# A two-layer hybrid trunk on one core: copying all of c out of its bank at once, and the row of rstd as two float32r products

## The chip, the cores and the metric

One Trainium2 chip, one core of it. The time is the device time of one launch in microseconds (us), the median of several runs. Beside it stands one profiled execution, from which every row of a trace in this document comes unless another kernel is named. The engines are called PE (TensorE, matrix products), DVE (VectorE), ACT (ScalarE), POOL (GpSimd) and SP (SyncE, which issues most transfers).

## What is computed

A trunk of two layers over 512 tokens of width 1024, all in float32. Each layer normalises its input, makes one combined projection of 3488 columns, feeds four groups of heads with it, multiplies each group's output by a SiLU gate, and projects back. Shortened from the reference:

```python
def hybrid_layer(x, ...):
    h = rmsnorm(x, norm_g)
    p = h @ w_in                                    # 512 x 3488
    (cq, ckv, kr, g_a, c_h, c_b, c_c, g_b, sg_u, sg_v, g_c, mq, mk, mv, g_d) = split(p)
    # A: latent attention, 4 heads; widths of cq, ckv, kr: 256, 128, 32
    q  = (rmsnorm(cq, mla_q_norm_g) @ mla_w_uq)     # 4 x 96
    kv = (rmsnorm(ckv, mla_kv_norm_g) @ mla_w_ukv)  # 4 x (64 + 64)
    k_rope = rope(rmsnorm(kr, mla_k_rope_g))
    ...
    o_a = causal_attention(q, k, v_a)
    o_b = c_b * short_conv(c_c * c_h, conv_w)       # B: width 3
    o_c = spatial_gate(sg_u, sg_v, ...)             # C: causal mixing in chunks of 128
    o_d = moba_attention(qd, kd, vd)                # D: blocks of 256, 4 heads
    y = concat([o_a*silu(g_a), o_b*silu(g_b), o_c*silu(g_c), o_d*silu(g_d)])
    return y @ w_out

def reference(x, ...):
    for l in range(2):
        x = x + hybrid_layer(x, ...)
    return x
```

## The kernel before

**Products.** A float32 operand is split into a high part in float32r and a low part, the rest, also float32r. A product of two such operands is three float32r products: high·high, low·high, high·low (names in the trace: `whi_`/`wlo_` for weights, `hTh`/`hTl` for the transposed input, `cTh`/`cTl` for transposed c). The high part is usually a copy on ACT, the low part a subtraction on DVE. A weight of 512 KB goes through the pool of `raw_` tiles, is split by halves, and waits there for its product. A few products are made in plain float32.

**The order of the work.** Nothing is left to an automatic scheduler. The program has a planner of its own, class `Order`: each piece of work is a generator (`Chain`) that yields due times, a heap picks the earliest, and the instruction is emitted when the planner's clock for its engine gets there. The clocks run on costs written in the program; there is one for each of ACT, DVE, POOL and the transfers, and `o.now` is the time of PE. So the order in which instructions stand on every engine is fixed when the program is built, and it changes as a whole if an operation is added, removed or made longer. All operations of ACT, DVE and POOL are emitted at one line, 178, and all products at line 208; the trace tells them apart by the names of their tiles. Buffers are handed out by `Slots` with `get` and `put`; `shared(slots, n)` is a `put` that acts at its n-th call. There are three accumulator banks of PSUM (`accS`), two for transposes and small things (`trS`), three for scores and other outputs (`sS`), and eleven SBUF tiles of 128x512 (`t2S`).

**Layer 0's beginning.** x is transposed in eight pieces on PE and split. Its norm is applied late: the projections are made of the unnormalised x (times the norm's gain), and the reciprocal root rstd, one number for each token, is multiplied onto what comes out. `x_stats` (line 765) sums the squares on ACT and makes rstd on POOL as a 128x4 array, token within a block by block. `x_row` (line 785) needs it along the free axis and on all partitions: POOL multiplies four identity blocks by the four columns of rstd (tile `rd`, 128x512), PE multiplies a block of ones with it (`rrow`, one float32 product of 512 columns), and ACT copies the bank, halved, to `rh` and its square behind it. `rh` is read by the gates and other outputs of layer 0. `ROWT`, 36,000 ns on the planner's clock, is when this is due.

**The low-rank part, c.** In layer 0 `c_first` (line 1704) makes the 416 columns of cq, ckv and kr for all four blocks of 128 tokens in four banks, three of `accS` and one of `sS`:

```python
home = [accS, accS, accS, sS]
...
if k == KT - 1:
    o.spawn(low_chain(L, t, a[t], o.now + PELAT, home[t]))
```

The banks fill in the order of the blocks, 0 and 1 together, then 2, then 3. For each of them `low_chain` (line 983) copies 384 columns to an SBUF tile `ct`, transposes them in three blocks (`cT`), splits the result (`cTh` on ACT, `cTl` on DVE) and makes q (six products of 384 columns) and kv (three of 512). Beside it `low_stats` (line 953) reads the same bank: three squares on ACT with their sums (32, 128 and 256 columns) and a copy of the last 32 columns to `krt`, on ACT too. The bank goes back when both are through with it. After that come small operations, a reciprocal root on POOL, and `krt`, scaled on DVE; when the last block is there, it is rotated and copied into K. The first product that asks for the first free bank of `accS` is `sq`, the projection of 512 columns to sg_v and mq, whose first split weights lie in the buffer `yTh`, `yTl`.
In layer 1 the same two functions run with one block at a time in `accS`.

**Behind that**, layer 0 runs the gates and projections of all groups between the attention heads: for each head of A scores (`sa`), a scaled and masked exponential (`pa`), transposes (`pTa`), a split (`pha`, `pla`) and the product with v (`oa`); for D the same with `sd`, `pd`, `pTd`, `phd`, `pld`, `od`. `gd` is D's gate, `zz` the product of c_c and c_h for the short convolution, and `oz`, `ox`, `oy` are the output projections, made as products of sums of blocks (as are layer 1's projections to sg_v, mq, mk and mv), with weights such as `whi_b`, `wlo_b`.

The functions that the change touches, with the line numbers of the profile:

Of the kernel before, what the change touches and what calls it, by code (L numbers as in the profile page):

```python
# [11 lines left out]
F32 = mybir.dt.float32  # L12
# [6 lines left out]
P = 128  # L19
S = 512  # L20
# [200 lines left out]
def hybrid_trunk(ctx: ExitStack, tc: tile.TileContext, x, positions, norm_g, w_c, w_f, w_t, w_o, mla_q_norm_g,  # L221
# [501 lines left out]
    xhi, xlo = ([Event() for _ in range(KT)] for _ in range(2))  # L723
    xsum = cst.tile([P, NT, KT // 2], F32, name="xsum")
    xv = cst.tile([P, 4, NT], F32, name="xv")
    v_ev, r_ev, rh_ev = Event(), Event(), Event()
    rh_box, rh_put = [], shared(hS, 14)
    RV, RR, RE, REE = range(4)
# [36 lines left out]
    def x_stats():  # L765
        ch = Chain(o)
        for kp in range(KT // 2):
            yield from ch.wait(xk_ev[2 * kp + 1])
            for t in range(NT):
                yield from ch.act(A.activation, junk[:, 0:2 * P], xk[kp][:, t, :], AF.Square, scale=D ** -0.5,  # L770
                                  accum_out=xsum[:, t, kp:kp + 1])
            c2 = Chain(o, ch.t)
            yield from c2.wait(xk_tr[2 * kp + 1])
            v4S.put(c2)
        yield from ch.dve(V.tensor_reduce, xv[:, RV, :], xsum, axis=AX.X, op=ALU.add)
        yield from ch.dve(V.tensor_scalar, xv[:, RV, :], xv[:, RV, :], 1.0, EPS, op0=ALU.mult, op1=ALU.add)
        t0 = ch.t
        for i, f in ((RE, EPS), (REE, EPS * EPS)):
            yield from ch.dve(V.tensor_scalar, xv[:, i, :], xv[:, RV, :], f, None, op0=ALU.mult)
        o.set(v_ev, ch.t)  # L780
        c2 = Chain(o, max(t0, ROWT))
        yield from pow_rstd(c2, xv[:, RR, :], xv[:, RV, :], NT)
        o.set(r_ev, c2.t)

    def x_row():

        ch = Chain(o)
        yield from ch.wait(r_ev)
        d = yield from t2S.get(ch, "rd")
        yield from ch.pool(G.tensor_tensor, d.rearrange("p (t c) -> p t c", t=NT),  # L790
                           ident.unsqueeze(1).to_broadcast([P, NT, P]),
                           xv[:, RR, :].unsqueeze(2).to_broadcast([P, NT, P]), op=ALU.mult)
        tp = yield from trS.get(ch, "rrow")
        yield from ch.pe(4 * cost(S), PE.matmul, tp, one_box[0][:, 0:P].bitcast(F32), d, start=True, stop=True)
        zz_put(ch)
        t2S.put(ch)
        rh_box.append((yield from hS.get(ch, "rh")))
        yield from ch.act(A.activation, rh_box[0][:, 0:S], tp, AF.Copy, scale=0.5)
        yield from ch.act(A.activation, rh_box[0][:, S:2 * S], tp, AF.Square, scale=0.5)
        trS.put(ch)  # L800
        o.set(rh_ev, ch.t)
# [149 lines left out]


    def low_stats(L, t, a, t0, done):
        ch = Chain(o, t0)
        ssq, krt = L.ssq, L.krt
        ct = L.ct[t]
        for i, (c0, c1) in enumerate(((384, 416), (256, 384), (0, 256))):
            yield from ch.act(A.activation, junk[:, :c1 - c0], a[:, c0:c1], AF.Square, scale=(c1 - c0) ** -0.5,
                              accum_out=ssq[:, t, 2 - i:3 - i])
        yield from ch.act(A.activation, krt[:, t, :], a[:, 384:416], AF.Copy)  # L960
        done(ch)
        m = sm.tile([P, 8], F32, tag="ms", name=f"ms{t}_{L.l}")
        e1, e2 = EPS, EPS * EPS
        if L.l == 0:
            yield from ch.wait(v_ev)
            e1, e2 = rv(RE, t), rv(REE, t)
        yield from ch.dve(V.tensor_scalar, m[:, 0:2], ssq[:, t, 1:3], 1.0, e1, op0=ALU.mult, op1=ALU.add)
        yield from ch.dve(V.tensor_scalar, L.e2[:, t, :], ssq[:, t, 0:2], EPS, e2, op0=ALU.mult, op1=ALU.add)
        yield from pow_rstd(ch, m[:, 4:6], m[:, 0:2], 2)
        L.ms[t] = m  # L970
        o.set(L.stat[t], ch.t)
        yield from ch.dve(V.scalar_tensor_tensor, krt[:, t, :], in0=krt[:, t, :], scalar=m[:, 5:6], in1=L.gr,
                          op0=ALU.mult, op1=ALU.mult)
        L.kr_left -= 1
        if L.kr_left:
            return
        yield from ch.wait(rope_ev)
        yield from rope(ch, krt, 16, cosT, sinT, f"k{L.l}")
        yield from ch.wait(L.QK_ev)
        yield from ch.pool(G.tensor_copy, L.K[:, :, :, 64:96], krt.unsqueeze(2).to_broadcast([P, NT, 4, 32]))  # L980
        o.set(L.kr_ev, ch.t)

    def low_chain(L, t, a, t0, slots):
        ch = Chain(o, t0)
        l = L.l
        done = shared(slots, 2)
        ct = yield from t2S.get(ch, f"ct{t}_{l}")
        L.ct[t] = ct
        o.spawn(low_stats(L, t, a, t0, done))
        if o.clk["A"] < o.clk["V"]:  # L990
            yield from ch.act(A.activation, ct[:, :384], a[:, :384], AF.Copy)
        else:
            yield from ch.dve(V.tensor_copy, ct[:, :384], a[:, :384])
        done(ch)
        tp = yield from trS.get(ch, f"cT{t}_{l}")
        for k in range(3):
            yield from ch.pe(109.0, PE.transpose, tp[:, k * P:(k + 1) * P], ct[:, k * P:(k + 1) * P], ident)
        t2S.put(ch)
        c_h = yield from t2S.get(ch, f"cTh{t}_{l}", F32R)
        c_l = yield from t2S.get(ch, f"cTl{t}_{l}", F32R)  # L1000
        yield from split2(ch, c_h[:, :384], c_l[:, :384], tp[:, :384])
        trS.put(ch)
        q_ps = yield from sS.get(ch, f"q{t}_{l}")
        for k in range(2):
            uq_h, uq_l = yield from unit(ch, f"uq_{l}", k)
            yield from mm3(ch, 384, q_ps[:, :384], c_h[:, k * P:(k + 1) * P], c_l[:, k * P:(k + 1) * P],
                           uq_h[:, k, :], uq_l[:, k, :], k == 0, k == 1)
        o.spawn(q_chain(L, t, q_ps, ch.t))
        uk_h, uk_l = yield from unit(ch, f"ukv_{l}")
        kv_ps = yield from sS.get(ch, f"kv{t}_{l}")  # L1010
        yield from mm3(ch, 512, kv_ps, c_h[:, 256:384], c_l[:, 256:384], uk_h[:, 0, :], uk_l[:, 0, :], True, True)
        t2S.put(ch)
        t2S.put(ch)
        L.up_left -= 1
        if L.up_left == 0:
            units[f"uq_{l}"].slots.put(ch)
            units[f"ukv_{l}"].slots.put(ch)
        yield from kv_chain(L, t, kv_ps, ch.t)
# [668 lines left out]
    def main():  # L1687
# [208 lines left out]
        early_put(m)  # L1896
        for L in layers:
            l = L.l
            L.ct, L.ms, L.up_left = {}, {}, NT
            L.kr_ev, L.kr_left = Event(), NT  # L1900
            L.vn_alloc = Event()
            L.md_alloc = {"mq": Event(), "mk": Event()}
# [106 lines left out]
    def start():  # L2009
        o.clk["D"] = 1000.0  # L2010
        cw = Chain(o)
        for kp in range(KT // 2):
            xk[kp] = yield from v4S.get(cw, f"x{kp}_0", [P, NT, 2 * P], F32)
        load_xk(0, 1)
        wp = yield from sS.get(cw, "warm")
        ones = one_box[0][:, 0:P].bitcast(F32)
        V.memset(ones, 1.0)
        A.activation(xsum[:, 0, 0:1], ones[:, 0:1], AF.Square, scale=D ** -0.5)
        o.fill = lambda: PE.matmul(wp[:, 0:P], ones, ones, start=True, stop=True)
        for _ in range(NWARM):  # L2020
            o.fill()
        PE.transpose(wp[:, 256:256 + NT + KT], junk[0:NT + KT, P:2 * P], ident[0:NT + KT, 0:NT + KT])
        V.tensor_copy(pg, wp[:, 256:256 + NT + KT])
        o.pe_end, o.fill_until = 3700.0, FILLEND
        o.clk["V"] = 3700.0

        def fill_end():
            o.fill_until = 0.0
            sS.put(Chain(o))
            return  # L2030
            yield
        o.spawn(fill_end(), FILLEND, -9)
        LOAD_HOOKS["c0_0"] = (lambda: load_xk(2, 4),)
        LOAD_HOOKS["c1_0"] = (lambda: load_xk(4, 6),)
        LOAD_HOOKS["c2_0"] = (lambda: load_xk(6, 8),)
        prow.append((yield from t2S.get(cw, "prow")))
        G.memset(prow[0][0:14, 0:P], 1.0)
        LOAD_HOOKS["sq0_0"] = (load_rows,)
        LOAD_HOOKS["sq1_0"] = (lambda: load_params(L0, 0),)
        LOAD_HOOKS["sq3_0"] = (lambda: load_params(L0, 1),)  # L2040
        o.spawn(param_cols(), COLT, 2)
        for u in order[:10]:
            u.wanted = True
        o.spawn(load_units(), None, 4)
        o.spawn(split_units(0, 4), None, LOPRIO)
        o.spawn(split_units(4, len(order)), None, 5)
        o.spawn(rope_tables(), 3700.0, 4)
        o.spawn(x_stats(), None, 5)
        o.spawn(x_row(), ROWT, 5)
        o.spawn(main(), None, 10)  # L2050
# [53 lines left out]
```

## Time and profile before

| | |
|---|---|
| median of 3 runs | 489.84 us (488.91 to 490.51) |
| profiled execution, its own time | 489.73 us |
| its span in the trace | 488.0 us |
| granted clock of PE | 0.999 |
| PE busy | 481.6 us, 99% of the span, 2432 products |
| DVE busy | 400.9 us, 82%, 893 instructions |
| ACT busy | 329.9 us, 68%, 898 instructions |
| POOL busy | 104.4 us, 21%, 172 instructions |

The span reaches from the first to the last instruction; the execution's own time has 1.7 us more around it. A row of the trace names the line, the engine, the operation, output<-inputs by the program's tile names and the shape; a number in square brackets is the time for which the engine had stood idle before the instruction, with what ended that. Products are pipelined and the ends of their records are modelled, so records overlap: the distance between the starts of two neighbours says more than the length of one.

### The profile page before, as it was taken

What the parts mean: (1) busy time and instruction counts of PE and PEld (TensorE: products, weight loads), DVE (VectorE), ACT (ScalarE), POOL (GpSimd) and SP (SyncE); (2) the same over time, 40 slices, a digit from 0 to 9 for tenths busy, and PEclk for the clock granted to TensorE, in tenths of its full rate; (3) what the DMA queues carried; (4) which work ended last, traced back from release to release, by engine and by line L of the source; (5) the groups of instructions that cost most, each with busy time, mean ns of one, the idle gap of its engine ahead of it and who ended that gap; (6) DMA issues with size and microseconds to landing.
All of it is one profiled execution on the core that took longest, in us unless ns stands there. A gap on an engine that the chain in (4) does not pass through costs nothing.

```text
span 488.0 us, 7509 instructions
## 1 busy us (share of the span) xinstructions
PE 481.6 (99%) x2432; PEld 408.9 (84%) x2432; DVE 400.9 (82%) x893; ACT 329.9 (68%) x898; POOL 104.4 (21%) x172
## 2 busy tenths in 40 slices
PE   9999999999999999999999999999999999999997
PEld 7988888888887888888889988888888888888786
DVE  3698487668987899789998688979788998997993
ACT  5896837677546766457667788769675687666650
POOL 7855330710051210000031013620402200000000
PEclk9999999999999999999999999999999999999999
DMA  8742335897499888596574186786832744427762
GB/s 263 249 135 78 124 128 218 225 197 162 151 330 240 208 217 218 188 343 224 199 239 145 65 290 250 165 246 177 209 131 85 153 136 146 173 66 258 253 242 89
DMA packets 41904, 92.89 MB, mean 190 GB/s; under 512 B 7158, under 2 KB 23048, under 8 KB 41480
## 3 DMA queue, kind: packets, MB, share of 16 engines
q1 hardware_dynamic: 29168, 79.82, 47.3%
q0 software_dynamic: 12672, 12.58, 16.7%
q8 instruction: 19, 0.31, 0.2%
q14 instruction: 21, 0.17, 0.1%
q10 hardware_dynamic: 24, 0.01, 0.0%
HBM read 84.53 MB, written 33.03 MB: 241 GB/s over the span
## 4 chain that ended last, share of the span: by engine, by line
PE 91%; DVE 3%; ACT 2%; DMA 2%; SPq 1%; issue 1%; ACTq 0%
PE oy L208 6%; PE cq L208 6%; PE kv L208 6%; PE gb L208 5%; PE su L208 5%; PE cc L208 5%; PE sq L208 5%; PE gc L208 5%; PE ch L208 5%; PE ga L208 4%; PE oz L208 4%; PE cb L208 4%; PE py L208 3%; PE ox L208 3%; PE sa L208 3%; PE gd L208 3%
## 5 line engine op out<-in xcount | busy, mean ns | idle before, releaser
L178 ACT ACTIVATE pa<-pa,mna 128x128 f32<-128x128 f32 (+3 forms) x53 | 27.8, 554 | 5.6 <-DVE mna L178 5.5
L178 ACT ACTIVATE pd<-pd,mnd 128x384 f32<-128x384 f32 (+3 forms) x49 | 25.8, 548 | 3.2 <-DVE mnd L178 2.9
L178 ACT ACTIVATE pha<-pTa 128x512 fp32r<-128x512 f32 (+3 forms) x32 | 13.9, 434 | 20.6 <-PE pTa L208 20.4
L178 ACT ACTIVATE phd<-pTd 128x512 fp32r<-128x512 f32 (+3 forms) x32 | 13.8, 434 | 16.1 <-PE pTd L208 15.9
L178 DVE CUSTOM_DVE_ANT_0 pa<-sa,maskb,rs_q 128x512 f32<-128x512 f32 (+3 forms) x32 | 16.6, 544 | 6.2 <-PE sa L208 3.2
L178 DVE TENSOR_TENSOR wlo_p<-raw_p,whi_p 128x512 fp32r<-128x512 f32 x28 | 19.1, 698 | 2.7 <-ACT whi_p L178 2.6
L178 ACT ACTIVATE whi_t<-raw_t 128x512 fp32r<-128x512 f32 x31 | 18.2, 619 | 4.5 <-DMA raw_t<-t 4.5
L208 PE MATMUL cq<-whi_c,hTh 128*128 128x416 f32 x64 | 20.8, 370 | 0.0
L178 DVE TENSOR_TENSOR wlo_t<-raw_t,whi_t 128x512 fp32r<-128x512 f32 x32 | 20.7, 679 | 0.0
L208 PE MATMUL cq<-wlo_c,hTh 128*128 128x416 f32 x64 | 20.0, 359 | 0.0
L178 DVE TENSOR_TENSOR pla<-pTa,pha 128x512 fp32r<-128x512 f32 (+3 forms) x32 | 15.4, 485 | 5.6 <-ACT pha L178 5.6
L208 PE MATMUL cq<-whi_c,hTl 128*128 128x416 f32 x64 | 19.8, 355 | 0.0
L178 POOL TENSOR_TENSOR rs_mk<-rs_mk,nhalf 128x16 f32<-128x16 f32 x2 | 6.5, 3243 | 56.3 <-DVE rs_mk L178 56.3
L178 DVE CUSTOM_DVE_ANT_0 pd<-sd,maskb,rs_mq 128x512 f32<-128x512 f32 (+3 forms) x32 | 17.0, 545 | 1.6 <-PE pTd L208 1.0
L178 DVE TENSOR_TENSOR pld<-pTd,phd 128x512 fp32r<-128x512 f32 (+3 forms) x32 | 15.1, 485 | 3.1 <-ACT phd L178 3.0
L178 POOL TENSOR_SCALAR xss<-xss 128x1 f32<-128x1 f32 x4 | 2.7, 668 | 69.6 <-ACT jk L178 65.3
L372 POOL DMA_DIRECT2D t<-in_w_o_dram x16 | 17.0, 1341 | 2.4 <-DMA t<-t 2.3
L178 DVE TENSOR_TENSOR wlo_b<-raw_b,whi_b 128x512 fp32r<-128x512 f32 x24 | 16.0, 682 | 0.1
L178 ACT ACTIVATE whi_b<-raw_b 128x512 fp32r<-128x512 f32 x23 | 13.9, 622 | 3.1 <-DMA raw_b<-in_w_o_dram 3.0
L178 ACT ACTIVATE whi_p<-raw_p 128x512 fp32r<-128x512 f32 x22 | 13.2, 625 | 3.9 <-DMA raw_p<-in_w_t_dram 3.9
L208 PE MATMUL pTd<-ident,pd 128*128 128x128 f32 x80 | 14.1, 272 | 0.6 <-ACT pd L178 0.6
L208 PE MATMUL pTa<-ident,pa 128*128 128x128 f32 x80 | 14.0, 273 | 0.0
(473 smaller groups left out, 1846.8 us busy)
## 6 DMA issues: line engine op xcount, KB each, us to landing
t<-in_w_o_dram POOLq DMA_DIRECT2D x16, 512.0 KB, 8.3
raw_t<-t SPq DMA_DIRECT2D x16, 512.0 KB, 4.0
raw_b<-in_w_o_dram SPq DMA_DIRECT2D x12, 512.0 KB, 4.0
t<-in_w_o_dram SPq DMA_DIRECT2D x8, 512.0 KB, 4.9
p<-in_w_t_dram POOLq DMA_DIRECT2D x8, 512.0 KB, 14.0
t<-t SPq DMA_DIRECT2D x8, 512.0 KB, 4.7
raw_p<-p SPq DMA_DIRECT2D x8, 512.0 KB, 3.2
ys<-ysc SPq DMA_DIRECT2D x14, 256.0 KB, 5.0
```

The costliest lines, as they stand in the source:

```text
L178: f(*a, **k)
L208: f(*a, **k)
L372: nc.gpsimd.dma_start(src(l, n, j), src(l, y, j), accum_op=ALU.add, max_dma_last_dim=1024)
```

## The change

Two edits. **c:** `low_chain` copies all 416 columns of the bank to `ct` and gives the bank back at once; `low_stats` starts after that and reads `ct`, so its squares come from SBUF, the copy to `krt` is gone, and the scaling of `krt` reads `ct` directly. The tile `ct` goes back when the transposes and `low_stats` are both through. **The row of rstd:** `x_stats` makes two parts of rstd with two small DVE operations, a copy in float32r and the rest; `x_row` builds a diagonal of each on POOL, in two tiles; `rrow` is two float32r products of a float32r block of ones with these, summed in the bank. The block of ones in float32r is written once, near the start.

```diff
@@ x_stats, x_row
+    xr2 = cst.tile([P, 2, NT], F32R, name="xr2")
...
         yield from pow_rstd(c2, xv[:, RR, :], xv[:, RV, :], NT)
+
+        yield from c2.dve(V.tensor_copy, xr2[:, 0, :], xv[:, RR, :])
+        yield from c2.dve(V.tensor_tensor, xr2[:, 1, :], xv[:, RR, :], xr2[:, 0, :].bitcast(F32), op=ALU.subtract)
         o.set(r_ev, c2.t)
...
-        d = yield from t2S.get(ch, "rd")
-        yield from ch.pool(G.tensor_tensor, d.rearrange("p (t c) -> p t c", t=NT),
-                           ident.unsqueeze(1).to_broadcast([P, NT, P]),
-                           xv[:, RR, :].unsqueeze(2).to_broadcast([P, NT, P]), op=ALU.mult)
+        d = []
+        for i, n in enumerate("hl"):
+            d.append((yield from t2S.get(ch, f"rd{n}", F32R)))
+            yield from ch.pool(G.tensor_tensor, d[i].rearrange("p (t c) -> p t c", t=NT),
+                               ident.unsqueeze(1).to_broadcast([P, NT, P]),
+                               xr2[:, i, :].bitcast(F32).unsqueeze(2).to_broadcast([P, NT, P]), op=ALU.mult)
         tp = yield from trS.get(ch, "rrow")
-        yield from ch.pe(4 * cost(S), PE.matmul, tp, one_box[0][:, 0:P].bitcast(F32), d, start=True, stop=True)
+        for i in range(2):
+            yield from ch.pe(cost(S), PE.matmul, tp, one_box[0][:, P:2 * P], d[i], start=i == 0, stop=i == 1)
         zz_put(ch)
+        t2S.put(ch)
         t2S.put(ch)
@@ low_stats, low_chain
-        yield from ch.act(A.activation, krt[:, t, :], a[:, 384:416], AF.Copy)
-        done(ch)
...
-        yield from ch.dve(V.scalar_tensor_tensor, krt[:, t, :], in0=krt[:, t, :], scalar=m[:, 5:6], in1=L.gr,
+        yield from ch.dve(V.scalar_tensor_tensor, krt[:, t, :], in0=a[:, 384:416], scalar=m[:, 5:6], in1=L.gr,
                           op0=ALU.mult, op1=ALU.mult)
+        done(ch)
...
-        done = shared(slots, 2)
+        done = shared(t2S, 2)
         ct = yield from t2S.get(ch, f"ct{t}_{l}")
-        L.ct[t] = ct
-        o.spawn(low_stats(L, t, a, t0, done))
         if o.clk["A"] < o.clk["V"]:
-            yield from ch.act(A.activation, ct[:, :384], a[:, :384], AF.Copy)
+            yield from ch.act(A.activation, ct[:, :416], a[:, :416], AF.Copy)
         else:
-            yield from ch.dve(V.tensor_copy, ct[:, :384], a[:, :384])
-        done(ch)
+            yield from ch.dve(V.tensor_copy, ct[:, :416], a[:, :416])
+        slots.put(ch)
+        o.spawn(low_stats(L, t, ct, ch.t, done))
         tp = yield from trS.get(ch, f"cT{t}_{l}")
...
-        t2S.put(ch)
+        done(ch)
@@ start
         V.memset(ones, 1.0)
+        V.tensor_copy(one_box[0][:, P:2 * P], ones)
```

More of the change, by code (lines that the diff above doesn't have):

```diff
@@ L955, in low_stats @@
         ssq, krt = L.ssq, L.krt
-        ct = L.ct[t]
         for i, (c0, c1) in enumerate(((384, 416), (256, 384), (0, 256))):
@@ L1898, in main @@
             l = L.l
-            L.ct, L.ms, L.up_left = {}, {}, NT
+            L.ms, L.up_left = {}, NT
             L.kr_ev, L.kr_left = Event(), NT
```

## The prediction

> **What bounds the kernel now.** I read the page first (busy times, chain), then the list of waits of the matrix engine, then the chain in order of time, then the timeline around each wait.
>
> ```profile
> PE 481.6 (99%) x2432; PEld 408.9 (84%) x2432; DVE 400.9 (82%) x893; ACT 329.9 (68%) x898; POOL 104.4 (21%) x172
> PE 91%; DVE 3%; ACT 2%; DMA 2%; SPq 1%; issue 1%; ACTq 0%
> ```
>
> ```profile
> PE warm L2019 <- DVE ones L2017: 1.1, 1, 1.1
> PE pTd L208 <- ACT pd L178: 0.6, 1, 0.6
> PE sq L208 <- ACT krt L178: 0.6, 1, 0.6
> PE gd L208 <- DVE zz L178: 0.3, 1, 0.3
> PE oz L208 <- DVE wlo_b L178: 0.3, 1, 0.3
> ```
>
> TensorE (PE) is busy 481.6 of 488.0 us and carries 91% of the chain that ended last. The second fence is its complete list of waits (us in total, times, longest): five, and only the third touches what is edited. So this kernel is one stream of products, and the change can be worth only (a) PE work that is taken out, and (b) those few waits, old ones that go and new ones that come. Three yardsticks follow, from the chain (start, us, what) and a group of transposes:
>
> ```profile
> 37.51 1.06 PE q L208 x6
> 90.28 0.44 PE pTa L208 x4
> 211.04 5.44 PE oz L208 x24
> ```
>
> A 128x512 product costs 5.44/24 = 0.227 us, a 384-column one 0.177, a transpose 0.11. Whatever two neighbouring starts lie further apart than this is lost, busy or not.
>
> **Part 1: the row of rstd.** The float32 product shows as two records, then the next products:
>
> ```profile
> 45.00 1.02 PE L208 MATMUL rrow<-rd,ones 128*128 128x512 f32 x2
> 45.46 0.80 PE L208 MATMUL sq<-yTh,hTh 128*128 128x512 f32 x1
> 46.10 0.40 PE L208 MATMUL sq<-yTl,hTh 128*128 128x512 f32 x1
> ```
>
> From 45.00 to 46.10 are 1.10 us, of which one sq product is 0.227: rrow took 0.87. Two float32r products at 0.227 take 0.45. PE gets 0.42 us back, on the path, whatever else happens. It also adds two DVE operations on 128x4 (the first makes the high part, the second subtracts it) and a second diagonal on GpSimd (POOL):
>
> ```profile
> 39.67 1.19 POOL L178 TENSOR_TENSOR rd<-ident,xv 128x512 f32<-128x512 f32 x1
> 39.28 2.13 DVE L178 TENSOR_TENSOR wlo_ga<-raw_ga,whi_ga 128x512 fp32r<-128x512 f32 x2
> L178 DVE TENSOR_TENSOR wlo_ga<-raw_ga,whi_ga x8: 671/681/1527, 39.3 to 296.5; 128x512 fp32r<-128x512 f32 x8
> ```
>
> The row is 1.19 us later on POOL; behind it there stand the copy of krt into K and the reciprocal roots for vn. The median wlo_ga takes 681 ns, the longest 1527, and that one ran while rd was being built: DVE lost 0.85 us beside it, so a second diagonal costs DVE some 0.85 more. The Trainium skill, "SBUF — State Buffer", section "SBUF: two separate sides", has a rule that speaks against the change here: a GpSimd operation and a DVE operation with two SBUF inputs exclude each other for a whole instruction, they do not share. The 1527 agrees with it.
>
> What hides this: at 40 to 46 us PE works on sq products whose operands are split already, the halves of ga that DVE is making are used after 61 us, and rh is read first by the gates, later still. So I price it at 0 on the path; with that cover gone it would be 0.85 for the diagonal, plus small change.
>
> **Part 2: the bank of c.** Before, cq's bank is returned when both the copy (384 columns) and low_stats are through, the last of which is ACT's copy of krt.
>
> ```profile
> 29.26 0.43 PE L208 MATMUL q<-whi_uq,cTh 128*128 128x384 f32 x1
> 30.65 0.49 PE L208 MATMUL cT<-ident,ct 128*128 128x128 f32 x3
> 31.74 0.50 PE L208 MATMUL sq<-yTh,hTh 128*128 128x512 f32 x1 [0.60 <-ACT krt L178]
> ```
>
> ```profile
> 28.82 0.76 ACT cTh L178 x2
> 31.60 0.10 ACT krt L178
> L178 ACT ACTIVATE krt<-cq x4: 198/208/222, 31.5 to 36.1; 128x32 f32<-128x32 f32 x4
> L178 DVE COPY ct<-cq x3: 543/544/545, 26.3 to 28.3; 128x384 f32<-128x384 f32 x3
> ```
>
> From the first q at 29.26 to sq at 31.74 are 2.48 us; the work in it is six q (1.06) and three transposes (0.33). Lost: 1.09 us. Now the first bank comes back with DVE's first copy, made from 26.3 on, so sq's wait ends 5 us before sq can start. Also, ACT no longer does the first token block's 128-column square and the second's 32-column one ahead of cTh, so cTh comes sooner, and kv0 is put where sq0 was. What is late next: cTl0, the low halves of ukv and cTl1, one behind the other on DVE, for q0, kv0 and q1, and ct3 on ACT for its transposes. I leave 0.2 of the 1.09 for them (0 to 0.5) and take 0.9. The copy is 32 columns wider; at 544/384 ns a column that is 45 ns, inside this bound. Eight krt copies of 208 ns leave ACT. In layer 1 the same bank comes back earlier too, but no wait of PE stands there: 0.
>
> The squares now read SBUF instead of PSUM:
>
> ```profile
> L178 ACT ACTIVATE junk<-cq 128x256 f32<-128x256 f32 x4 | 1.6, 390 | 0.0
> L178 ACT ACTIVATE squaresk<-K x5: 401/403/437, 48.3 to 290.5; 128x256 f32<-128x256 f32 x5
> ```
>
> 390 ns from PSUM, 403 from SBUF at the same size: 24 squares cost ACT 0.3 us, less than the 1.7 us of copies that go. The Trainium skill, "Perfetto Trace Analysis", section "Optimizing Scalar/DVE Operations", puts the fixed access cost of the scalar engine at about 93 ns on SBUF and 51 on PSUM; by that 24 squares would cost 1.0 us, an estimate of that page. The rows decide, and either hides beside PE.
>
> Tiles: ct stays in its t2 tile until krt is scaled, some 5 us longer, and two t2 tiles hold the diagonals. Eleven exist. No row shows a wait for one; I take 0, at most 0.5.
>
> **Part 3: the whole order moves.** The kernel orders its instructions by its own due times, so everything behind shifts, which the order listing shows. In layer 0 the attention heads stand 20 to 30 products (4 to 7 us) earlier among PE's products, SP issues the residual's xr2 and xr3 ahead of two weight loads, in layer 1 xr0 and xr1 too. So the three late waits must each be looked up.
>
> ```profile
> 148.47 6.53 DMA raw_cc<-in_w_f_dram
> 156.14 1.85 ACT pd L178 x4
> 157.17 0.27 PE L208 MATMUL pTd<-ident,pd 128*128 128x128 f32 x1
> 158.04 0.55 PE L208 MATMUL pTd<-ident,pd 128*128 128x128 f32 x3 [0.60 <-ACT pd L178]
> ```
>
> 157 us: pTd starts 0.87 apart, 0.76 lost: ACT stood 2.7 us at whi_cc for raw_cc, with pd behind it. Now pd stands ahead of whi_cc on ACT: that wait goes. But raw_cc's load is then issued as late as before, and DVE's half of whi_cc stands ahead of pld, which od needs; if it lands in 6.5 us again, od waits about 0.6. Net gain 0.1 (0.76 gained to 1.0 lost).
>
> ```profile
> 342.69 0.39 PE L208 MATMUL cc<-hTh,wlo_cc 128*128 128x512 f32 x1
> 343.86 0.50 PE L208 MATMUL gd<-hTh,whi_gd 128*128 128x512 f32 x1 [0.35 <-DVE zz L178]
> 457.62 0.61 PE L208 MATMUL oz<-whi_b,yD 128*128 128x512 f32 x2
> 458.50 0.50 PE L208 MATMUL oz<-wlo_b,yD 128*128 128x512 f32 x1 [0.26 <-DVE wlo_b L178]
> 458.83 0.40 PE L208 MATMUL oz<-whi_b,yD 128*128 128x512 f32 x1
> ```
>
> 343 us: 1.17 from cc to gd, less 0.227 and four transposes (0.44): 0.50 lost to zz. In the new order nine score products (three each of 512, 384 and 256 columns) stand between cc's end and pTa, so gd comes about 1.5 us later and zz is there. Gain 0.5.
> 458 us: 0.88 less two products, and 0.33 less one: 0.53 lost to wlo_b's second half, which stood behind ys, suml and xr on DVE. Now both halves stand together, and od's last product is 49 products (11.1 us) ahead of the consumer where it was 37 (8.4 us). Gain 0.5.
>
> New waits: the clearest place is layer 0's first head.
>
> ```profile
> 83.94 0.75 DVE L178 TENSOR_SCALAR hi1a<-t1a,pcol 96x512 fp32r<-96x512 f32 x1 [1.25 <-PE t1a L208]
> 87.06 1.92 ACT L178 ACTIVATE pa<-pa,mna 128x128 f32<-128x128 f32 x4 [1.00 <-DVE mna L178]
> ```
>
> From hi1a's start to the end of pa's scaling DVE and ACT take 5.0 us. PE has 21 full products and the scores of one head (1.57, as chain entries of nine show) there now, 6.3 us; in the new order 15, 5.0 us. The spare of 1.3 us is used up. I take 0.5 (0 to 1.5) for this and others like it.
>
> **Sum**, against the profiled execution of 489.73 us (span 488.0 and 1.7 around it; 0.1 below the median of 489.84): -0.9 (bank) -0.42 (row) -0.1 (157) -0.5 (343) -0.5 (458) +0.5 (new) = -1.9. That is 487.8, on the median's scale **487.9 us**, 0.4% faster. About 0.3%, 1.47 us, is what a measurement of this kernel can tell from no change: below 488.4 is faster, above 491.3 slower.
>
> **Rivals.**
> *Late waits only change places.* The two edits pay 1.3, and what 343, 157 and 458 give back returns elsewhere. For it: DVE is 82% busy and every wait is a chance meeting. 489.84 - 1.3 = 488.5.
> *The vector engine becomes the bound in layer 0's heads* (the slower side).
>
> ```profile
> 90.00:120.00 30.00, 30.00 (x170) 25.86 (x169) 21.00 (x55) 22.27 (x65) 10.04 (x9) 1.00 1.05 199
> 120.00:150.00 30.00, 30.00 (x151) 25.12 (x151) 27.36 (x58) 15.70 (x30) 8.94 (x8) 1.00 0.72 221
> ```
>
> (Columns: window, length, then PE, PEld, DVE, ACT, POOL busy.) Heads come 4 to 7 us earlier against PE's products, while DVE's list loses 2 us in all; at 120 to 150 us DVE works 27.4 of 30. If each of the eight heads in layer 0 loses the 0.6 that pd lost, 4.8 stand against gains of 2.4: 492.2. It decides from 0.5 a head on. Against it: at 90 to 120 DVE is idle 9 us, and in the whole of both windows PE shows no wait.
> *GpSimd's second diagonal holds DVE where PE needs it* (the rule of the SBUF page): 0.85 and POOL's own 1.19 are not hidden, of which at most 1.2 reaches PE: 489.1.
> *The bank is not what holds sq:* the wait is taken over by cTl1, ct3 or the low half of ukv, only rrow's 0.42 stays: 489.4.
>
> **How the numbers follow.** Forecast 0.55; waits change places 0.17; DVE bound 0.18; diagonal 0.05; bank 0.05. The second lies so near the bound that I count 0.05 of it as faster. Faster 0.60, same 0.22, slower 0.18. Range: if no new wait comes and 157's goes whole, -3.1 (486.7); 486.6 to 490.9 leaves out a little below and most of the slower case.
>
> **What would show it.** Right: no wait of sq on ACT before 32 us; two rrow products of 0.23; no gd on zz, no oz on wlo_b; PE's span shorter by what its list of waits lost. Wrong: a wait of PE on pd, pa, pla or mna over 0.5 us in 80 to 205 us, several of them; a long wlo of DVE beside rdh and rdl with PE waiting for it.

## The result, and the profile after

The changed kernel takes 493.48 us (median of 7 runs, 490.96 to 494.92) where the kernel before takes 489.84 (7 runs, 488.91 to 490.51): a ratio of 1.0063, with a 95% interval of 1.0045 to 1.0081. It is slower by 0.6%, where 0.4% faster was forecast, and it lies above the forecast's range. The profiled execution took 491.76 us with a span of 490.1, 2.0 us above before's 489.73. So some 1.7 us of the median's time (493.48 less 491.76) are not in this profile; e2 and e4 below show what they are.

Busy times of the changed kernel, from the page:

```profile
PE 481.1 (98%) x2432; PEld 408.9 (83%) x2432; DVE 400.1 (82%) x887; ACT 335.2 (68%) x929; POOL 105.0 (21%) x173
```

Its complete list of waits of the matrix engine (us in total, times, longest):

```profile
PE py L208 <- ACT hi0a L178: 2.3, 1, 2.3
PE warm L2026 <- DVE ones L2023: 1.1, 1, 1.1
PE pTd L208 <- ACT pd L178: 1.0, 1, 1.0
PE kv L208 <- DVE wlo_kv L178: 0.5, 1, 0.5
PE sd L208 <- DVE mnd L178: 0.3, 1, 0.3
PE oy L208 <- DVE suml L178: 0.2, 1, 0.2
```

The four waits that were to go (sq on krt, pTd on pd at 157 us, gd on zz, oz on wlo_b) are gone. Five others stand in their place, and one of them, 2.3 us at 329 us, is larger than any of before's. PE is busy 0.5 us less and the span is 2.1 us longer.

The two edits themselves did what they were for. The products where the first bank's wait was, and the row, in the timeline of PE after:

```profile
28.96 0.33 PE L208 MATMUL q<-whi_uq,cTh 128*128 128x384 f32 x1
...
29.53 0.44 PE L208 MATMUL q<-whi_uq,cTl 128*128 128x384 f32 x1
...
32.65 0.47 PE L208 MATMUL sq<-yTh,hTh 128*128 128x512 f32 x1
...
47.46 0.39 PE L208 MATMUL rrow<-rdh,ones 128*128 128x512 f32 x1
47.68 0.39 PE L208 MATMUL rrow<-rdl,ones 128*128 128x512 f32 x1
47.91 0.39 PE L208 MATMUL sq<-whi_sq,hTh 128*128 128x512 f32 x1
```

sq has no wait any more, and the row takes 0.45 us from 47.46 to 47.91. The two diagonals for it held DVE, as the prediction feared. POOL's two products, and DVE's operations on `krt` in that stretch (shortest, median and longest of each pair in ns):

```profile
40.26 1.04 POOL L178 TENSOR_TENSOR rdh<-ident,xr 128x512 fp32r<-128x512 f32 x1 [1.65 <-DVE xr L178]
42.33 1.36 POOL L178 TENSOR_TENSOR rdl<-ident,xr 128x512 fp32r<-128x512 f32 x1 [1.03 <-DVE xr L178]
L178 DVE TENSOR_TENSOR krt<-krt,cosT x2: 214/595/976, 40.4 to 41.3; 128x64 f32<-128x64 f32 x2
L178 DVE TENSOR_TENSOR krt<-krt,rbk x2: 216/466/717, 43.1 to 45.3; 128x64 f32<-128x64 f32 x2
```

The first of each pair started beside a diagonal (at 40.41 and 43.06 us), took 976 and 717 ns, and ended 0.08 us after the diagonal did; the second of each took 214 and 216. DVE lost 0.76 and 0.50 us by that, and PE nothing: its lost time from 40 to 50 us, by the measure that follows, is 0.02.

To see where the rest went, take for every product the distance to the next start, less its own time (0.227 us for 512 columns, 0.187 for 416, 0.174 for 384, 0.117 for 256, 0.108 for a transpose), and add it up by stretch. This lost time, in us, is used for all kernels below; layer 1 begins near 250 us, and a lower clock counts as lost time too:

| stretch of the span | before | after | difference |
|---|---|---|---|
| 0 to 20 (start) | 3.8 | 3.5 | -0.3 |
| 20 to 50 (both edits) | 2.2 | 1.1 | -1.1 |
| 50 to 250 (layer 0) | 2.5 | 4.5 | +1.9 |
| 250 to the end (layer 1) | 3.5 | 5.0 | +1.5 |

The edits win 1.1 us where they are made, and more is lost far behind them. Each figure is of one execution: for 50 to 250 us, programs with the same order in layer 0 differ by up to 0.9 (e1 and e4 below).

**Where it is lost.** The chain in order of time, after, in three windows of layer 0 (start, us, what):

```profile
79.79 0.75 DVE hi1a L178
80.54 0.61 DVE wlo_kv L178
...
81.19 0.96 PE kv L208 x3
...
149.43 5.15 DMA raw_cc<-in_w_f_dram
...
154.60 0.43 DVE whi_cc L178
...
155.63 0.39 DVE pd L178
...
181.40 6.84 DMA raw_gc<-in_w_f_dram
...
188.26 0.63 ACT whi_gc L178
188.89 1.82 ACT pd L178 x4
...
190.76 0.66 PE pTd L208 x4
```

In the first no load is late: kv waits for the low half of its weight, which stands behind hi1a on DVE. The second and third have one form: the load of a weight lands after 5.2 and 6.8 us, the conversion of that weight stands on DVE or ACT already and holds its engine until then, and an attention head's scaling, for which PE waits next, stands behind it.

Layer 1's large one is the same on three engines at once. The load in the chain of after, then the timelines of POOL, ACT, DVE and PE around it:

```profile
317.24 9.55 DMA sgw<-in_sg_w_dram
```

```profile
326.86 0.64 POOL L178 TENSOR_SCALAR_AFFINE_SELECT sgw<-sgw 128x512 f32<-128x512 f32 x1 [4.92 <-DMA sgw<-in_sg_w_dram]
327.54 0.63 ACT L178 ACTIVATE wsh<-sgw 128x512 fp32r<-128x512 f32 x1 [2.83 <-POOL sgw L178]
...
327.86 0.55 POOL L178 TENSOR_TENSOR bmv<-bmv,nhalf 128x1 f32<-128x1 f32 x1
328.45 0.48 DVE L178 SCALAR_TENSOR_TENSOR vn<-vn,bmv,lb_b 128x256 f32<-128x256 f32 x1 [3.28 <-POOL bmv L178]
...
331.26 0.68 DVE L178 TENSOR_TENSOR x<-py,x 128x512 f32<-128x512 f32 x1
331.46 0.57 ACT L178 ACTIVATE hi0a<-t0a 96x512 fp32r<-96x512 f32 x1
...
332.09 0.47 PE L208 MATMUL py<-whi_p,yTh 128*128 128x512 f32 x1 [2.30 <-ACT hi0a L178]
```

sgw, the spatial gate's own weight, takes 9.6 us to land. POOL stands at its masking, ACT at its conversion, and DVE at vn, whose root (bmv) stands behind the masking on POOL: 3.28 us. Five operations behind vn comes x<-py, which empties the bank of the product before; PE's next py needs that bank and starts 0.15 us after it. The profile names hi0a, which happened to end 0.06 us before PE started; e5 shows below that it was not hi0a. Before, the load landed as late, and POOL stood even longer for it:

```profile
326.45 1.15 POOL L178 TENSOR_SCALAR_AFFINE_SELECT sgw<-sgw 128x512 f32<-128x512 f32 x1 [14.00 <-DMA sgw<-in_sg_w_dram]
...
328.07 0.68 DVE L178 TENSOR_TENSOR x<-py,x 128x512 f32<-128x512 f32 x1
328.67 0.47 DVE L178 SCALAR_TENSOR_TENSOR vn<-c,bmv,lg_b 128x256 f32<-128x256 f32 x1
```

But there x<-py stood ahead of vn on DVE, and wsh came on ACT at 335.82 only, so nothing that PE needed was behind it. The planner takes a transfer to land after its bytes divided by 360, in ns, plus 2 us (the cost in the program): 2.7 us for sgw and 3.5 for a weight of 512 KB. The new order stands as early as the planner believes.

### The profile page after: what moved, and what is told of

Its sections match the earlier page's. It is cut to its first block, busy times and chain, and to the rows that moved or that the text cites. A ratio compares the mean times of both kernels' runs of the same rounds, so it can differ in the third digit from the quotient of the medians.

```text
span 490.1 us, 7538 instructions
## 1 busy us (share of the span) xinstructions
PE 481.1 (98%) x2432; PEld 408.9 (83%) x2432; DVE 400.1 (82%) x887; ACT 335.2 (68%) x929; POOL 105.0 (21%) x173
## 4 chain that ended last, share of the span: by engine, by line
PE 81%; DVE 9%; DMA 4%; ACT 3%; issue 1%; POOL 0%; SPq 0%; DVEq 0%
PE cq L208 6%; PE oy L208 6%; PE kv L208 6%; PE gb L208 5%; PE gc L208 5%; PE su L208 5%; PE sq L208 4%; PE ga L208 4%; PE cc L208 3%; PE cb L208 3%; PE sa L208 3%; PE ch L208 3%; PE oz L208 3%; PE gd L208 2%; PE pz L208 2%; PE px L208 2%
## 5 line engine op out<-in xcount | busy, mean ns | idle before, releaser
L178 ACT ACTIVATE pa<-pa,mna 128x384 f32<-128x384 f32 (+3 forms) x59 | 30.5, 549 | 2.9 <-DVE mna L178 2.8
L178 POOL TENSOR_TENSOR rs_mq<-rs_mq,nhalf 128x16 f32<-128x16 f32 x2 | 5.9, 2926 | 42.7 <-ACT pha L178 21.5
```

Of the source, the lines that this page charges most:

```text
L178: f(*a, **k)
```

## The experiments

**The theory:** the edits are worth what was forecast, and the loss is the order's. The planner moves hundreds of instructions, and the new order meets a few late inputs early. **Rivals:** the edits cost by themselves (tiles held longer, squares from SBUF, the second diagonal); DVE is the bound, so that waits only change places; the granted clock is lower.

**e1 to e4: which edit, which layer.** The bank edit can be made in one layer alone, by keeping both versions of `low_chain` and `low_stats`. The order of the built programs then falls into blocks: e3 has the changed kernel's order in layer 0, row for row, and before's in layer 1; e4 has e1's in layer 0 and the changed kernel's in layer 1.

```diff
# e1: only x_stats, x_row and the block of ones are changed; e2: only low_stats and low_chain
# e3: both edits, layer 1 with the old functions
-                o.spawn(low_chain(L, t, a, o.now + PELAT, accS))
+                o.spawn(low_chain_b(L, t, a, o.now + PELAT, accS))
# e4: both edits, layer 0 with the old functions
-                    o.spawn(low_chain(L, t, a[t], o.now + PELAT, home[t]))
+                    o.spawn(low_chain_b(L, t, a[t], o.now + PELAT, home[t]))
```

> Only the row of rstd is changed, c as before. The planner's order stays as before in layer 1 and moves 503 of PE's rows in layer 0. Order theory (the edits pay what was forecast, the loss of the changed kernel lies in waits that the new order of layers 0 and 1 brings): 0.42 us for the row, layer 1 with before's waits, layer 0's own order unknown by up to 1 us: 489.4, between 488.4 and 490.4; no wait of py on hi0a near 329 us. Clock theory (a part of the loss, some 1.5 us, is a lower granted clock that comes with the two float32r products of the row): 491, with clocks of 0.995 to 0.997 in its runs. Cost theory (the second diagonal holds DVE): 490.7, with a long wlo beside rdh or rdl and PE waiting behind it.

> Only c is changed, in both layers; the row is one float32 product as before. Its order is within 173 of PE's rows the one of the changed kernel. Order theory: the changed kernel's waits (py on hi0a 2.3 us, pTd on pd 1.0) are mostly there, plus 0.42 for the row: 492 to 494. Clock theory: clocks of 0.999 as before, 491.9 to 492.3, the changed kernel's profiled time and the row. Cost theory of the row: about 490, most of the loss gone.

> The row, and c in layer 0 alone; layer 1 reads and returns the bank as before. Its order is the changed kernel's in layer 0, row for row, and before's in layer 1. Order theory: layer 0 as in the changed kernel's trace, which is 0.55 us longer there than before (1.4 won at 20 to 50 us, 1.95 lost behind it), layer 1 as before, without the 2.3 us of py on hi0a: 490.3. Cost theory (the early return and the longer hold of the tile cost by themselves wherever they are used): the loss of layer 0 remains and layer 1 shows nothing, as above, so only the split between e3 and e4 tells: half of the loss in each.

> The row, and c in layer 1 alone. Its order is that of e1 in layer 0 and the changed kernel's in layer 1, row for row. Order theory: e1 plus what layer 1 lost in the changed kernel's trace, 1.5 us (2.5 at 329 us, 0.5 at 471, less the 1.1 won at 343 and 458): 490.9, with py waiting on hi0a for about 2.3 us behind the load of sgw. Cost theory: the edit in layer 1 takes no PE time, so as e1.

| kernel | median us (runs) | ratio to before, 95% | lost 20-50 | 50-250 | 250-end | runs at a clock of 0.997 or less |
|---|---|---|---|---|---|---|
| before | 489.65 (35) | | 2.2 | 2.5 | 3.5 | 0 |
| e1 row alone | 489.34 (12) | 0.9987, 0.9974 to 1.0000 | 2.0 | 2.9 | 3.7 | 0 |
| e2 bank alone | 491.79 (12) | 1.0049, 1.0021 to 1.0077 | 1.7 | 2.3 | 6.3 | 5 |
| e3 row, bank in layer 0 | 491.02 (12) | 1.0024, 1.0010 to 1.0038 | 1.1 | 4.4 | 3.9 | 0 |
| e4 row, bank in layer 1 | 490.89 (12) | 1.0023, 1.0009 to 1.0037 | 2.0 | 2.0 | 6.4 | 3 |

e1 and e4 came out as the order theory said (489.4 and 490.9), e2 a little below its range, e3 0.7 us above the forecast. The losses follow the orders: e3 has the changed kernel's 4.4 in layer 0 and not its layer 1; e4 has py on hi0a (2.1 us) with e1's layer 0. From e1, the bank edit in layer 0 costs 1.7 us and in layer 1 1.6; together with e1 that makes 492.6, inside the changed kernel's interval (489.84 times 1.0045 to 1.0081, 492.0 to 493.8). That a bank edit in layer 1, where PE had no wait for the bank, costs 1.6 us, speaks already for the order. So does e2's layer 0: it has the bank edit too, in an order of its own since the row is missing, and loses 2.3 there, no more than before. And e2 has the lower clock in five runs without the row's two products, while e1 with them has it in none, so these products are not what lowers it.

**The missing 1.7 us.** e2 and e4 lost 6.3 and 6.4 us in layer 1, the changed kernel 5.0 in its profile. Four stretches of e4, then one of the changed kernel (window, length, busy PE, PEld, DVE, ACT, POOL, then the granted clock, the DMA share and GB/s):

```profile
328.00:330.00 2.00, 0.67 (x3) 0.21 (x2) 2.00 (x5) 2.00 (x8) 0.14 (x1) 1.00 0.59 80
330.00:332.00 2.00, 1.20 (x4) 1.00 (x5) 2.00 (x5) 1.97 (x7) 0.00 (x0) 0.79 1.11 177
332.00:334.00 2.00, 2.00 (x6) 1.57 (x5) 2.00 (x5) 1.95 (x7) 0.00 (x0) 0.50 0.04 5
334.00:336.00 2.00, 2.00 (x9) 1.59 (x8) 2.00 (x4) 1.29 (x7) 0.00 (x0) 0.86 0.71 190
```

```profile
332.00:334.00 2.00, 1.91 (x8) 1.61 (x9) 2.00 (x5) 1.97 (x7) 0.00 (x0) 1.00 0.85 131
```

Behind the gap PE runs at half its clock in e4, from 331.15 to 334.57 us, with its products 0.43 us apart instead of 0.23; in the changed kernel's profile it does not. So the gap costs its 2 us, and in some runs 1.7 us on top (lost time from 330 to 340 us: 1.8 in e2 and e4, 0.1 in the changed kernel's profile). The changed kernel's runs agree, but for one: those at a clock of 0.995 or 0.997 took 493.48, 494.07 and 494.92, those at 0.999 or 1.000 took 490.96, 491.51, 491.76 and 493.54. Why the last is so slow is not known.

Why only some runs have it can be read from the traces. In each of the twelve profiles the granted clock changes only at whole steps of 3.41 us, counted from its first change to full clock near the start. In e4 that change is at 6.89 us, and half clock lasts from step 95 (331.15) to step 96 (334.57). What counts is how long PE stood within one step. e4's gap (328.67 to 330.80) lies whole in the step before, 2.13 us; of e2's gap 1.91 us lie in one step, and e10's two gaps lie in one, 1.77 us together. The gap of the changed kernel's profile is longer, 2.30 us from 329.79, but a step ends at 330.95 and cuts it into 1.16 and 1.14: the clock stays. In all twelve profiles, with the idle time after the last product counted too, half clock followed each of the 11 steps in which PE stood 1.77 us or more, and none of those in which it stood 1.51 or less. Where the steps lie is a chance of the start (the first change came between 4.35 and 7.09 us), so the profiled run was lucky.

The Trainium skill, "TensorE: Matmul & The Clock Gate", section "Part 1: The HAM clock gate (the "warmup" mystery)", has PE fall to half its rate after an idle window of about 3.4 us, windows that run freely. The traces agree on the length of the slow stretch (3.41 us) and on windows that run freely. They do not agree that the whole window must be idle: 1.77 us in it sufficed here.

**e5: only the load is moved.** Layer 1's sgw is issued earlier on SP, and its place in the plan is kept, so that no instruction of PE, ACT, DVE or POOL moves.

```diff
         if L.stok:
-            yield from ch.wait(L.mix_go)
+            yield 285000.0
         sgw = yield from obS.get(ch, f"sgw{l}")
         sgw = sgw.rearrange("p (g s) -> p g s", g=4)
-        dma(ch, P * 2048, sgw, sg_w[l])
+        if L.stok:
+            nc.sync.dma_start(sgw, sg_w[l])
+            yield from ch.wait(L.mix_go)
+            ch.t = max(ch.t, o.now) + 3900.0
+        else:
+            dma(ch, P * 2048, sgw, sg_w[l])
```

> The changed kernel, with the one load of layer 1's sgw issued some 16 us earlier on SP; no instruction of PE, DVE, ACT or POOL stands in another place. Order theory, with the late load as its means (ACT stands at wsh, behind it hi0a): the 2.3 us of py on hi0a at 329 us go, and with them the stretch of half clock that e2 and e4 show behind that gap and that the single run of the changed kernel's profile does not: 489.3 (491.76 of the profiled run less 2.5), clocks of 0.999 to 1.000 in all runs, and a spread like that of before, 2 us instead of 4. Cost theory (the longer hold of tiles, squares from SBUF): 493 as the changed kernel.

Measured: 489.64 us (11 runs, 488.67 to 491.50; ratio 0.9993, 0.9979 to 1.0007, to before's 489.83). The same operations in e5's timelines:

```profile
321.14 0.95 POOL L178 TENSOR_SCALAR_AFFINE_SELECT sgw<-sgw 128x512 f32<-128x512 f32 x1
...
324.86 0.62 ACT L178 ACTIVATE wsh<-sgw 128x512 fp32r<-128x512 f32 x1
325.33 0.48 DVE L178 SCALAR_TENSOR_TENSOR vn<-vn,bmv,lb_b 128x256 f32<-128x256 f32 x1
...
328.14 0.68 DVE L178 TENSOR_TENSOR x<-py,x 128x512 f32<-128x512 f32 x1
328.77 0.58 ACT L178 ACTIVATE hi0a<-t0a 96x512 fp32r<-96x512 f32 x1
328.97 0.47 PE L208 MATMUL py<-whi_p,yTh 128*128 128x512 f32 x1
```

POOL, ACT and DVE no longer wait at these operations. py starts at 328.97, 0.15 us after x<-py again, while hi0a ends at 329.35: the releaser was x<-py, and the expectation's "behind it hi0a" is corrected by that. The lost time of layer 1 is 2.7 us where before has 3.5 (e5's profiled execution is the fastest of its runs), and every run has a clock of 0.999 or 1.000. The median is 0.3 above the forecast, and the spread 2.8 us. One load, issued 16 us earlier, takes 3.8 us off the changed kernel's median (3.4 by the two ratios to before). The edits' own cost cannot explain that, since both edits are still in; and with the gap the lower clock is gone too.

**e6 and e7: layer 0's two.** On top of e5, the planner is told that layer 0's weights of the gated features land later.

```diff
+LATE = 1000.0        # e6; e7: 2500.0
...
-            o.set(u.loaded, ch.t)
+            o.set(u.loaded, ch.t + (LATE if u.name[:3] in FEATS and u.name[-1] == "0" else 0.0))
```

> As e5, and the planner takes layer 0's weight loads of the gated features (ga to gd) to land 1 us later than before. That moves 36 of PE's rows in layer 0; on ACT the conversion of gc's last weight goes behind the scaling of pd in the last head, that of cc's is no longer on DVE ahead of pd of the second. Order theory: pTd on pd at 189 us (1.1) and sd on mnd at 155 us (0.5) go or become smaller: 487.7 to 488.3. Rival (layer 0 is bound by DVE, the waits only change places): as e5.

> As e6 with 2.5 us instead of 1, which moves 264 of PE's rows and takes all of these conversions off DVE and behind the heads' scalings. Order theory: the same two waits go, others may come from the new order: 487.5 to 489. Rival (bound by DVE): as e5 or above.

e6: 488.45 us (11 runs; ratio 0.9970, 0.9960 to 0.9980), just above its range. e7: 487.01 us (5 runs, 486.84 to 487.35; ratio 0.9945, 0.9932 to 0.9959), below its range. The whole list of PE's waits in e7:

```profile
PE warm L2032 <- DVE ones L2029: 1.1, 1, 1.1
PE oy L209 <- DVE suml L179: 0.3, 1, 0.3
PE kv L209 <- ACT Q L179: 0.2, 1, 0.2
```

How much hangs on the two loads can be read without e6: the changed kernel, e3 and e5 have the same order in layer 0, and their loads took different times. raw_gc landed after 6.84, 6.40 and 5.98 us, and ahead of pTd at 189 us PE lost 1.13, 0.69 and 0.26. raw_cc landed after 5.15, 5.73 and 5.51, and ahead of sd at 155 us PE lost 0.50, 1.06 and 0.85. What the load takes longer, PE loses, within 0.02 us. So the wait of pTd was nearly gone in e5 already, by chance.

e6 traded the wait of sd for one of pTd (0.7, near 154 us). e7 has neither, and kv on wlo_kv at 80 us is gone too; layer 0 from 50 us on loses 1.8, where e5 lost 3.8 and before 2.5. DVE has no less to do in it (busy 401.8 us, 400.1 in the changed kernel), so DVE was not the bound. e7 beats both kernels, before by 2.8 us, with the two edits, the early load and the planner's 2.5 us together.

**e8: a moved order and nothing else.** The kernel before, with the planner's cost of `rrow` halved; the product stays one of float32.

```diff
-        yield from ch.pe(4 * cost(S), PE.matmul, tp, one_box[0][:, 0:P].bitcast(F32), d, start=True, stop=True)
+        yield from ch.pe(2 * cost(S), PE.matmul, tp, one_box[0][:, 0:P].bitcast(F32), d, start=True, stop=True)
```

> The kernel before with nothing changed but the planner's cost of rrow, which it takes for half as long; the product stays one of float32. 488 of PE's rows move in layer 0, none in layer 1, nearly as in e1. Order theory (a moved order costs only where a load is met early): e1 plus the 0.42 us of the row: 489.8, no wait above 0.6 us but those of before. Rival (any moved order loses about 1 us, because the order of before was a lucky one): 490.5 or more.

Measured: 489.78 us (11 runs; ratio 1.0001, 0.9990 to 1.0012). Here 488 rows of PE moved at no cost, so a new order is not worse in itself. e1, with nearly that order and the two products, took 0.44 us less, about the price of the row. That is weak evidence: the two were measured apart, each against its own before they differ by 0.26, and the intervals are wider than either.

**e9: the planner's 2.5 us without the change.** The kernel before with e7's `LATE`, in layer 0.

> The kernel before, with the planner's 2.5 us for layer 0's loads as in e7 and nothing else; layer 1 keeps before's order. It tells whether e7's gain is the planner's alone. Order theory: the wait of pTd on pd at 157 us (0.76 lost) may go, new ones may come; the edits' own 1.3 (0.4 row, 0.6 to 0.9 bank) and the 0.8 that layer 1's order gains are missing: 488.5 to 490. Rival (the whole of e7's gain is the planner's 2.5 us): 487.

Measured: 490.15 us (11 runs; ratio 1.0007, 0.9998 to 1.0016), just above the forecast's range and far from the rival's 487. The wait of pTd at 157 us went, and others came (waits of PE in e9's profile, which is of its slowest run, 491.52):

```profile
PE py L209 <- DVE x L179: 0.9, 1, 0.9
...
PE kv L209 <- DVE wlo_kv L179: 0.5, 1, 0.5
PE pTa L209 <- DVE u L179: 0.4, 1, 0.4
```

So e7's gain is not the planner's figure alone. The kernel before with e5's early load as well was not run; in before's profile PE did not wait behind that load.

**e10: the same in layer 1 too.** On top of e7.

```diff
-... if u.name[:3] in FEATS and u.name[-1] == "0" else 0.0))
+... if u.name[:3] in FEATS else 0.0))
```

> As e7, with the 2.5 us in layer 1 too. e7's trace has no wait on a load left in layer 1, so by the order theory nothing is to be had: 486.8 to 488, the 0.5 us of oy on suml at 466 may move. If loads met early still cost PE where the list of waits shows nothing: 486.5 or less.

Measured: 489.40 us (11 runs; ratio 0.9995, 0.9985 to 1.0005), 2.4 above e7: the forecast was wrong. The largest of PE's waits in e10, and PE's timeline there:

```profile
PE ox L209 <- DVE wlo_t L179: 1.8, 2, 0.9
```

```profile
463.64 0.50 PE L209 MATMUL ox<-wlo_t,yD 128*128 128x512 f32 x1 [0.83 <-DVE wlo_t L179]
...
464.29 0.63 PE L209 MATMUL ox<-whi_t,yTh 128*128 128x512 f32 x1
464.71 0.63 PE L209 MATMUL ox<-wlo_t,yTh 128*128 128x512 f32 x1
```

Weights taken to land later are converted later, and now the last ones are late for the output product: two gaps of 0.94 and 0.83 us, and the half clock again (products 0.42 apart; 4 of 11 runs at 0.997 or less). The order theory itself allows that, but the forecast had again looked only at the waits of the trace at hand. A truer figure for loads is no cure by itself; e7 is an order that happens to meet nothing, found with two edits, not a rule.

## Why the prediction was wrong

- **The row, 0.42.** Right: lost time from 40 to 50 us fell by 0.49 (0.51 to 0.02). The prediction gave DVE 0.85 us for each diagonal, hidden from PE; the two took 0.76 and 0.50 and were hidden. They fell on krt's operations and not on wlo_ga, whose longest is 693 ns in the changed kernel. This agrees with the rule that the prediction cites from the Trainium skill, "SBUF — State Buffer", section "SBUF: two separate sides".
- **The bank, 0.9.** Right in its means, a third too much: 0.58 (lost 20 to 50 us fell by 1.07, less the row's 0.49). 0.57 from the first q with cTh to the first with cTl, where two products take 0.35, is the 0.2 that was left for cTl0; what was also counted as waiting, and stays, is 0.09 to 0.12 at each change of bank. The squares from SBUF cost ACT 22 to 26 ns more each (a square of 128x256 takes 414 ns where it took 392), 0.6 us for the 24 and not 0.3, and nothing of it reached PE.
- **157 us, -0.1.** The mechanism came as told: raw_cc late (5.2 us), DVE's half of whi_cc holding a head. It was sd on mnd that waited rather than od, 0.50 instead of 0.6, and 0.26 was gained. That is one execution's figure: with the same order sd lost 1.06 in e3 and 0.85 in e5, which would be a small loss.
- **343 and 458 us, -0.5 each.** Right: both waits are gone, 0.52 and 0.56 us of lost time with them, and they go with the bank edit in layer 1 (in e2 and e4, not in e1 and e3).
- **New waits, +0.5 (0 to 1.5).** The step that failed: this term of the sum, for waits that the new order brings, was priced at 0.5 and at most 1.5. They cost 4.7 in the profiled run: 0.68 at 80 us, 1.13 at 189, 2.46 at 329, 0.45 at 471. The first is the place that the prediction chose, layer 0's first head, though it was the low half of kv's weight behind hi1a and not the head itself. For the others it had looked up only the places where before waited, and priced the rest of a moved order as one chance. What it should have asked at every load is whether a conversion now stands ahead of the load's landing, and who is behind it: the row of sgw with POOL's 14.00 us was in before's trace.
- **A gap's second price.** The prediction had none. Where PE stood 1.77 us or more within one step of the clock, half clock followed and cost 1.7 us. By their mean clock that came in three of the changed kernel's seven runs, the median run among them, and not in the profiled run.
- **The rivals.** "The late waits change places" had the direction of it and too small a size. "The vector engine becomes the bound" had the sign, and its 492.2 lies within the measured interval by luck: its means, 0.6 us at each of eight heads, did not come, and nothing took work off DVE in e7. "The bank is not what holds sq" is refuted by the rows above. The second diagonal held DVE, as its rival said, but not where PE needed it.

Why the bank edit in layer 1 makes the planner put vn and wsh ahead was not tried; that it does is shown by e3 and e4.

The sum, with what was measured: -0.58, -0.49, -0.26, -0.52, -0.56 and +4.7 make +2.3 for the profiled run, -0.3 by a chance of the start, against the 2.0 that it took; and 1.7 for the clock. The five gains add up to 2.41 where the prediction has 2.42. That is luck, since the bank came 0.32 short and the other four made up for it. Without the new waits, e7 is at 487.01, 0.9 below the forecast of 487.9.

## What to carry to other kernels

In a kernel whose order is planned as a whole, an edit's own worth can be the smaller part: list every transfer that is slower than the planner believes, and for each the first instruction that needs it, its place on its engine in the new order, and who stands behind it. That is to be done for all loads of the program and not only where the old order waited, since a load that lands late costs nothing until something moves ahead of it. A loss that appears far from an edit is found by undoing the edit stage by stage, and shown by moving the late input alone, with all other instructions kept in place.

## What the runs showed of the hardware

The granted clock changed only at steps of 3.41 us. Half clock followed a step in which PE stood 1.77 us or more in all (11 such steps in twelve profiles), and none in which it stood 1.51 us or less; the limit between them was not measured. So e10's two gaps of 0.94 and 0.83 us in one step were followed by it, and the changed kernel's 2.30 us, cut in two by the end of a step, were not. By the mean clock of all runs, 0.997 or less came in 15 of the 42 runs of the four kernels with such gaps (the changed kernel, e2, e4, e10), and in none of the 73 runs of the other seven variants, whose lowest was 0.998.

Two DVE operations with krt among their inputs started beside a POOL product of 128x512 and ended with it: 976 and 717 ns instead of 214 and 216. Not every DVE operation does: one that reads the bank of sq (BATCH_NORM_STATS2, at 42.72 us, beside `rdl`) took 0.41 us, and 0.43 before with no POOL product beside it.

A transfer of 256 KB (sgw) took 9.6 us in layer 1, while two of POOL's accumulating transfers, issued at 309.2 and 309.9 us, were under way until 321.6 and 327.7. Issued 16 us earlier it took 5.6, and the same transfer in layer 0 of the changed kernel 3.9. What slowed it was not tried.
